# Five instead of three seven-product pairs in three gate blocks, thirteen instead of ten in the last product, with part of the weight sums added up in DRAM

## The chip, the cores and the metric

The kernel runs on one core of one Trainium2 chip. TensorE (PE in the profile, PEld its weight loads) multiplies, VectorE (DVE), ScalarE (ACT) and GpSimd (POOL) work on tiles in SBUF, and transfers are issued by SyncE (SP), ACT and POOL and carried out by the core's 16 DMA engines. The metric is the device time of one execution in microseconds; the profile is of one execution.

## The reference, cut to what matters

A two-branch decoder layer: 256 tokens, width 2048, feed-forward width 5632, all in float32.

```python
z = h @ w_in                                   # heads of both branches and two gates of 2048 columns
g_a, g_m = sigmoid(z[..., OFF_GA:OFF_GM]), sigmoid(z[..., OFF_GM:D_IN])
merged = g_a * (a_out @ w_proj_a) + g_m * (m_out @ w_proj_m)
x = x + merged @ w_out
u = causal_dwconv(rmsnorm(x) @ w_up)           # gate and value halves of 5632
x = x + (silu(u_gate) * u_val) @ w_down        # the last product: 256 x 5632 by 5632 x 2048
```

## The kernel before, in words

**Stages.** The weights are streamed once, in the order of use: the mLSTM gates (names `mog`), queries, keys and values of attention (`fq`, `fk`, `fv`), those of the mLSTM (`mq`, `mk`, `mv`), the two branch gates in four blocks of 1024 columns (`g0` to `g3`), the two projections (`p`), the output product (`wo0`, `wo1`), the up product (`up`) and the last product in two blocks of 1024 columns (`y0`, `y1`).

**A weight's way.** All weights are cut into chunks of 128 partitions by up to 2048 float32, 1 MiB at most. `load_chunk` (L124) has SP load a chunk into one of three `raw` buffers. `split_sub` (L134) splits a piece of a chunk, 1024 columns as a rule, into a high part `wh` (ACT, L170: a rounded copy) and a low part `wl` (DVE, L171: the difference); there are four buffers of each. A product is then three matmuls: low activation by `wh`, high activation by `wh`, high activation by `wl` (`prod`, L290). `next_sub` (L178) hands PE the next piece and has the pieces up to three ahead split, so a split waits for one of three things: its chunk, a free buffer, its engine.

**Pairs.** In the gate blocks, `wo` and `y`, a chunk is a pair of row blocks: 2 x 128 rows of the weight by two halves of 512 columns, a 2 x 2 matrix of blocks b12, b11, b22, b21 in the order of the chunk's columns. With the two token halves this is a 2 x 2 by 2 x 2 block product. A plain pair ("p" in the patterns of L37 to L39) takes eight products in two pieces, 24 matmuls of 512 columns. A pair of kind "S" takes Strassen-Winograd's seven products, 21 matmuls, from four pieces of 1024, 512, 1024 and 1024 columns: `b` (b11, b22), `b21`, `t13` and `t24`. For it DVE makes four sums of weight blocks in a tile `sums` (L155, L162, L165), and the activations have four sums of their own: for the gates `gate_sums` (L633) makes them once, from the normalised activations `hN`, into `gs` tiles; for `y` the up stage makes them (`put_sums`, L217), POOL stores them to `s_dram` (L949) and `load_sums` (L959) brings them back through POOL into two `s_ops` buffers, 768 KB for two pairs.

**Order around the change.** SP's, POOL's and the engines' queues run in order. In the `fq`/`fk` stage POOL also computes the inverse roots `qc` (L444) that DVE needs (L596); in the first gate block the same for the mLSTM heads (`nc`). The first gate block has plain pairs only, and its pieces run the tasks of the mLSTM and, at its end, `gate_sums`. In each block the last two pairs are plain, and the results of the seven products are put together on DVE during them.

Of the kernel before, what the change touches and what calls it, by code (L numbers as in the profile page):

```python
# [60 lines left out]
def trunk(ctx: ExitStack, tc: tile.TileContext, a):  # L61
# [57 lines left out]
    add_pairs(a["w_dn"], [Y_PAIRS] * 2)  # L119

# [13 lines left out]
    def split_sub(j):  # L134
        if j >= len(subs_of) or j in subs:
            return
        i, s, kind = subs_of[j]
# [3 lines left out]
        n = 512 if kind == "b21" else chunks[i][1] // 2  # L141
        raw, sums = raws[i], s_tiles.get("sums")


        if kind == "whole":
            src = raw[:, s * n : (s + 1) * n]
        elif kind == "b":
            src = raw[:, 512:1536]
# [4 lines left out]

            with tc.issue_after(last_of["wl"].ins):
                nc.vector.tensor_tensor(  # L155
                    sums[:, :1024].rearrange("p (i c) -> p i c", i=2),
                    raw[:, :512].unsqueeze(1).to_broadcast([P, 2, 512]),
                    src.rearrange("p (i c) -> p i c", i=2), ALU.subtract,
                )
        elif kind == "b21":  # L160
            src = raw[:, 1536:]
            nc.vector.tensor_tensor(sums[:, 1024:1536], raw[:, 1024:1536], sums[:, :512], ALU.subtract)  # L162
        elif kind == "t13":
            src = sums[:, :1024]
            nc.vector.tensor_tensor(sums[:, 1536:], raw[:, 1536:], sums[:, 1024:1536], ALU.subtract)  # L165
# [4 lines left out]
        nc.scalar.activation(wh[:, :n], src, AF.Copy)  # L170
        last_of["wl"] = nc.vector.tensor_tensor(  # L171
            wl[:, :n], src, wh[:, :n].bitcast(F32), ALU.subtract
        )
# [43 lines left out]
    def put_sums(src, dst, keep):  # L217

        a11, a21, a12, a22 = (src[:, i * P : (i + 1) * P] for i in range(4))
        n = 4 if keep else 3
# [4 lines left out]
        nc.vector.tensor_tensor(s1, a21, a22, ALU.add)
        nc.vector.tensor_tensor(s2, s1, a11, ALU.subtract)
        nc.vector.tensor_tensor(s4, a12, s2, ALU.subtract)
        put(dst[0], dst[1], sv)  # L230
# [52 lines left out]
    def s_block(name, pairs, s_ops, pattern, pools, dst, add=True, per_piece=0):  # L283
# [3 lines left out]
        ps, late, left = {}, [], pattern.count("S")  # L287
# [15 lines left out]
        def tt(o, x, y):  # L303
            late.append(lambda: nc.vector.tensor_tensor(o, x, y, ALU.add))

        for m, kind in enumerate(pattern):
# [34 lines left out]
            c11, c12, c21, c22 = (dst(tok, h) for tok in range(2) for h in range(2))  # L341
            u2 = scratch("u2", [P, 512])
            if add:
# [9 lines left out]
                tt(c22, c22, u3)
            else:
# [55 lines left out]
    def when_there(x):  # L410

        return nc.gpsimd.tensor_copy(mhalf[:, :1], x[:, :1].bitcast(F32))
# [204 lines left out]
    g_sums = [m for m, kind in enumerate(G_PAIRS) if kind == "S"]  # L617
# [315 lines left out]
    for j in range(NF):  # L933
# [12 lines left out]
        if Y_PAIRS[m] == "S":  # L946
# [9 lines left out]
    s_pos = [m for m, kind in enumerate(Y_PAIRS) if kind == "S"]  # L956
    ring = []

    def load_sums():  # L959

        i = len(ring) % (N_S // 2) * 12 * P
        if len(ring) < N_S:
            ring.append(a8(f"s_ops{len(ring)}", [12 * P], F32R))
            nc.gpsimd.dma_start(ring[-1], s_dram[:, i : i + 12 * P])

    def sums_of(b, m):
# [3 lines left out]
        at = [ring[r][:, q * P : (q + 1) * P] for q in range(6 * i, 6 * i + 6)]  # L970
# [92 lines left out]
```

## Time and profile before

| | |
|---|---|
| runs | 1378.11 us median of 3 (1377.85 to 1378.25) |
| profiled execution | 1378.12 us, of which its span is 1376.3 us |
| busy, share of the span | PE 99%, PEld 84%, DVE 78%, ACT 56%, POOL 3% |
| granted TensorE clock | 0.999 |
| moved by DMA | 281.76 MB: SP's queue 260.20 MB in 53.0% of the 16 engines' time, POOL's queue 20.38 MB in 4.4% |
| POOL | 73 instructions that count as busy |

The span is what the hardware profiler recorded of the program; 1.8 us of the execution lie around it. Busy PE counts time in which a matmul is under way. A row of the windows gives, for one stretch, its length, each engine's busy time with the number of instructions, the granted clock, the share of DMA time and the rate.

### The profile page before, as it was taken

The numbers are of one execution on the slowest core, as the hardware profiler recorded it, in microseconds if no ns is written. First come the engines' busy times: TensorE is split into PE (matmuls) and PEld (weight loads), VectorE is DVE, ScalarE is ACT, GpSimd is POOL, SyncE is SP. The second block draws the span as 40 slices with busy tenths as digits, with TensorE's granted clock in tenths as the row PEclk, the third lists the DMA queues.
The fourth block names the chain that finished last, engine by engine and source line by source line (L and its number), as shares of the span: only waits on it lengthen the run. The fifth ranks groups of instructions, "written<-read, shape, count | busy, mean of one in ns | idle before, by whom it ended". The sixth has DMA issues, their size and how long they took to land.

```text
span 1376.3 us, 18405 instructions
## 1 busy us (share of the span) xinstructions
PE 1368.2 (99%) x6934; PEld 1160.8 (84%) x6934; DVE 1078.2 (78%) x1539; ACT 770.9 (56%) x1102; POOL 40.9 (3%) x73
## 2 busy tenths in 40 slices
PE   9999999999999999999999999999999999999998
PEld 8878888888888888888888888888888888888887
DVE  5655766556888866899888888878888889889887
ACT  6655554445665544465756555556555556554553
POOL 2101000000000000000000000000000000000000
PEclk9999999999999999999999999999999999999999
DMA  9644554543555556465655555555555566768853
GB/s 324 237 180 166 182 206 153 172 155 132 189 209 186 215 213 231 177 231 200 210 207 192 195 195 199 203 199 198 196 195 189 205 239 222 257 241 277 298 192 120
DMA packets 44073, 281.76 MB, mean 205 GB/s; under 512 B 5008, under 2 KB 5024, under 8 KB 13264
## 3 DMA queue, kind: packets, MB, share of 16 engines
q1 hardware_dynamic: 39168, 260.20, 53.0%
q0 software_dynamic: 4672, 20.38, 4.4%
q8 instruction: 54, 0.88, 0.3%
q14 instruction: 35, 0.29, 0.1%
q10 hardware_dynamic: 144, 0.02, 0.0%
HBM read 272.45 MB, written 8.13 MB: 204 GB/s over the span
## 4 chain that ended last, share of the span: by engine, by line
PE 97%; issue 1%; DMA 1%; POOL 1%; DVE 0%; SPq 0%; ACT 0%; DVEq 0%; ACTq 0%; POOLq 0%
PE up L233 36%; PE p L233 6%; PE y1q L233 6%; PE y0q L233 6%; PE fq L233 3%; PE g0q L233 3%; PE mv L233 3%; PE fk L233 3%; PE fv L233 3%; PE wo0q L233 2%; PE g3q L233 2%; PE g2q L233 2%; PE g1q L233 2%; PE wo1q L233 2%; PE y1p L233 2%; PE y0p L233 2%
## 5 line engine op out<-in xcount | busy, mean ns | idle before, releaser
L170 ACT ACTIVATE wh<-raw 128x1024 fp32r<-128x1024 f32 (+2 forms) x496 | 498.2, 1015 | 407.2 <-PE up L233 109.6
L171 DVE TENSOR_TENSOR wl<-raw,wh 128x1024 fp32r<-128x1024 f32 (+2 forms) x496 | 574.0, 1167 | 189.5 <-ACT wh L170 184.7
L233 PE MATMUL up<-h,wh 128*128 128x512 f32 x1408 | 442.6, 396 | 0.0
L233 PEld LDWEIGHTS up<-h,wl 128*128 128x128 f32 x1408 | 264.4, 188 | 62.4
L233 PE MATMUL up<-h,wl 128*128 128x256 f32 x1408 | 276.6, 278 | 0.0
L233 PEld LDWEIGHTS up<-h,wh 128*128 128x128 f32 x1408 | 214.6, 189 | 0.4 <-DVE h L202 0.2
L170 ACT ACTIVATE wh<-sums 128x1024 fp32r<-128x1024 f32 x70 | 74.3, 1062 | 119.8 <-PE y1q L233 36.0
L171 DVE TENSOR_TENSOR wl<-sums,wh 128x1024 fp32r<-128x1024 f32 x70 | 85.5, 1221 | 43.9 <-ACT wh L170 43.8
L921 DVE SCALAR_TENSOR_TENSOR t<-u,cst,t 128x256 f32<-128x256 f32 x176 | 84.7, 481 | 3.7 <-ACT t L919 0.7
L233 PE MATMUL p<-wh,am 128*128 128x512 f32 x256 | 79.6, 392 | 0.0
L233 PE MATMUL y0q<-wh,ghl 128*128 128x512 f32 x232 | 71.5, 389 | 0.0
L233 PE MATMUL y1q<-wh,ghl 128*128 128x512 f32 x232 | 71.4, 389 | 0.0
L233 PEld LDWEIGHTS p<-wh,am 128*128 128x128 f32 x256 | 47.6, 188 | 9.7
L919 ACT ACTIVATE t<-u,cst 128x256 f32<-128x256 f32 x88 | 52.2, 593 | 1.7 <-DVE u L916 1.7
L233 PEld LDWEIGHTS y1q<-wh,ghl 128*128 128x128 f32 x232 | 43.5, 188 | 9.0
L233 PEld LDWEIGHTS y0q<-wh,ghl 128*128 128x128 f32 x232 | 43.5, 188 | 8.9
L233 PE MATMUL p<-wl,am 128*128 128x512 f32 x128 | 49.9, 390 | 0.0
L233 PE MATMUL y0q<-wl,ghl 128*128 128x512 f32 x116 | 45.1, 389 | 0.0
L233 PE MATMUL y1q<-wl,ghl 128*128 128x512 f32 x116 | 45.1, 389 | 0.0
L155 DVE TENSOR_TENSOR sums<-raw 128x1024 f32<-128x1024 f32 x35 | 42.6, 1217 | 0.0
L233 PE MATMUL mog<-wh,hT 128*128 128x348 f32 (+1 forms) x192 | 41.2, 324 | 1.3 <-ACT wh L170 0.9
L233 PE MATMUL g0q<-wh,hN 128*128 128x512 f32 x128 | 41.2, 401 | 0.0
(370 smaller groups left out, 2041.8 us busy)
## 6 DMA issues: line engine op xcount, KB each, us to landing
raw<-in_w_up SPq DMA_DIRECT2D x88, 1024.0 KB, 4.8
raw<-in_w_dn SPq DMA_DIRECT2D x44, 1024.0 KB, 5.2
raw<-in_w_g SPq DMA_DIRECT2D x32, 1024.0 KB, 4.8
raw<-in_w_fox SPq DMA_DIRECT2D x24, 1024.0 KB, 4.9
raw<-in_w_p SPq DMA_DIRECT2D x16, 1024.0 KB, 4.9
raw<-in_w_out SPq DMA_DIRECT2D x16, 1024.0 KB, 4.8
raw<-in_w_mqk SPq DMA_DIRECT2D x8, 1024.0 KB, 4.8
raw<-in_w_mv SPq DMA_DIRECT2D x8, 1024.0 KB, 4.8
```

The lines of the kernel that those rows point to most:

```text
L155: nc.vector.tensor_tensor(sums[:, :1024].rearrange("p (i c) -> p i c", i=2), raw[:, :512].unsqueeze(1).to_broadcast([P, 2, 512]), src.rear ...
L170: nc.scalar.activation(wh[:, :n], src, AF.Copy)
L171: last_of["wl"] = nc.vector.tensor_tensor(wl[:, :n], src, wh[:, :n].bitcast(F32), ALU.subtract)
L233: last_of["mm"] = nc.tensor.matmul(out, lhsT, rhs, start=start, stop=stop)
L919: nc.scalar.activation(t, u[:, 2:], AF.Identity, scale=w[2], bias=w[3])
L921: nc.vector.scalar_tensor_tensor(out=t, in0=u[:, i : i + S], scalar=w[i], in1=t, op0=ALU.mult, op1=ALU.add)
```

## The change

The pattern of gate blocks 1 to 3 goes from `pSpSpSpp` to `pZSZSZpp`, that of `y` from `p`, ten times `Sp`, `p` to `p`, six times `SZp`, `Zpp`. "Z" is a seven-product pair like "S", with the same four pieces for PE, whose weight sums are not made by DVE: a tile `t` of 1 MiB in DRAM per pair holds them (9 for the gates, 14 for `y`, 23 in all). The pair then takes two chunks in place of one: 768 KB of the weight itself (b11, b22, b21) and 1 MiB of `t`.

`sums_in_dram` makes a `t` in six transfers from POOL's queue, DRAM to DRAM, three of which add to what stands at their destination: b12 to two quarters, b11 and b22 added to them, the first sum copied to the third quarter, b22 added, that copied to the fourth, b21 added. Each needs the landing of the one before. `plan` places them at every second chunk from the beginning of `fox` (`fq`) and of `wo`, so that a gate tile is begun every 4 chunks and a `y` tile every 6; `begin_steps` ties a place to the chunk's first split by a one-column copy on ACT (`marks`) and one on POOL (`seen`), behind which POOL issues the transfers.

The signs of the sums are turned so that they can be made by additions: DVE's instructions stay what they were, with other operations. `gate_sums` makes five sets instead of three, the fifth in the buffer `mv`. `load_sums` brings the two pairs of an `s_ops` buffer in two transfers of 384 KB.

```diff
-G_PAIRS = "pSpSpSpp"
+G_PAIRS = "pZSZSZpp"
-Y_PAIRS = "p" + "Sp" * 10 + "p"
-N_S = Y_PAIRS.count("S")
+Y_PAIRS = "p" + "SZp" * 6 + "Zpp"
+N_S = len(Y_PAIRS) - Y_PAIRS.count("p")
...
+            if kind == "Z":
+                t = dram.tile([P, 2048], F32, name=f"t{len(z_sums)}")
+                z_sums.append((t, ap[i]))
+                add_chunk(ap[i][:, 512:], 1536, (1024, 1536))
+                add_chunk(t, 2048)
+            else:
+                add_chunk(ap[i], 2048, ("b", "b21", "t13", "t24") if kind == "S" else None)
...
+    def sums_in_dram(i):
+        t, w = z_sums[i]
+        q = lambda x, n: x[:, n * 512 : (n + 1) * 512]
+        b12, b11, b22, b21 = (q(w, n) for n in range(4))
+        put_to = lambda o, x: lambda: nc.gpsimd.dma_start(o, x)
+        add_to = lambda o, x: lambda: nc.gpsimd.dma_start(o, x, accum_op=ALU.add)
+        return [
+            put_to(
+                t[:, :1024].rearrange("p (i c) -> p i c", i=2),
+                b12.unsqueeze(1).to_broadcast([P, 2, 512]),
+            ),
+            add_to(t[:, :1024], w[:, 512:1536]),
+            put_to(q(t, 2), q(t, 0)), add_to(q(t, 2), b22),
+            put_to(q(t, 3), q(t, 2)), add_to(q(t, 3), b21),
+        ]
...
+    def plan(source, name, apart):
+        c0 = next(i for i, c in enumerate(chunks) if c[2] == name)
+        mine = [i for i, (_, w) in enumerate(z_sums) if w.tensor.name == a[source].tensor.name]
+        for n, i in enumerate(mine):
+            for step in range(6):
+                c = c0 + 2 * (apart * n + step)
+                j = next(j for j, x in enumerate(subs_of) if x[0] == c)
+                steps_at.setdefault(j, []).append((i, step))
+    plan("w_g", a["w_fox"].tensor.name, 2)
+    plan("w_dn", a["w_out"].tensor.name, 3)
...
+    def begin_steps(j, x):
+        mark = marks[:, list(steps_at).index(j) :][:, :1]
+        nc.scalar.activation(mark, x[:, :1].bitcast(F32), AF.Copy)
+        with tc.issue_after(when_there(mark).ins):
+            for i, step in steps_at[j]:
+                sums_in_dram(i)[step]()
...
         nc.scalar.activation(wh[:, :n], src, AF.Copy)
+        if j in steps_at:
+            begin_steps(j, wh)
...
     def when_there(x):
-        return nc.gpsimd.tensor_copy(mhalf[:, :1], x[:, :1].bitcast(F32))
+        return nc.gpsimd.tensor_copy(seen, x[:, :1].bitcast(F32))
...
         if i % 2 == 0:
-            g_ops["tile"] = a8(f"gs{i}", [2, 2, 512], F32R)
+            last = big.tile([P, 2, 2, 512], F32R, tag="mv", name="gs4") if i == 4 else None
+            g_ops["tile"] = last or a8(f"gs{i}", [2, 2, 512], F32R)
...
-            ring.append(a8(f"s_ops{len(ring)}", [12 * P], F32R))
-            nc.gpsimd.dma_start(ring[-1], s_dram[:, i : i + 12 * P])
+            ring.append(a8(f"s_ops{len(ring)}", [2, 6 * P], F32R))
+            for n in range(2):
+                i = (2 * len(ring) - 2 + n) % N_S * 6 * P
+                nc.gpsimd.dma_start(ring[-1][:, n], s_dram[:, i : i + 6 * P])
```

Two places show how the instructions move. The first is DVE in the middle of gate block 1. Before, a plain pair's two low parts stand ahead of an "S" pair's sums and four low parts:

```order
L171 TENSOR_TENSOR wl_3310<-raw_3261,wh_3309 128x1024
L171 TENSOR_TENSOR wl_3317<-raw_3261,wh_3316 128x1024
L155 TENSOR_TENSOR sums_3142<-raw_3297 128x1024
L171 TENSOR_TENSOR wl_3328<-raw_3297,wh_3327 128x1024
L162 TENSOR_TENSOR sums_3142<-raw_3297,sums_3142 128x512
L171 TENSOR_TENSOR wl_3341<-raw_3297,wh_3340 128x512
L165 TENSOR_TENSOR sums_3142<-raw_3297,sums_3142 128x512
L171 TENSOR_TENSOR wl_3358<-sums_3142,wh_3357 128x1024
L171 TENSOR_TENSOR wl_3376<-sums_3142,wh_3375 128x1024
```

The same place now, where a "Z" pair's four low parts (from two `raw` buffers) stand ahead of the second "S" pair of the block:

```order
L228 TENSOR_TENSOR wl_3417<-raw_3380,wh_3416 128x1024
L228 TENSOR_TENSOR wl_3424<-raw_3380,wh_3423 128x512
L228 TENSOR_TENSOR wl_3434<-raw_3404,wh_3433 128x1024
L228 TENSOR_TENSOR wl_3446<-raw_3404,wh_3445 128x1024
L210 TENSOR_TENSOR sums_3371<-raw_3443 128x1024
L228 TENSOR_TENSOR wl_3457<-raw_3443,wh_3456 128x1024
L217 TENSOR_TENSOR sums_3371<-raw_3443,sums_3371 128x512
L228 TENSOR_TENSOR wl_3467<-raw_3443,wh_3466 128x512
L220 TENSOR_TENSOR sums_3371<-raw_3443,sums_3371 128x512
L228 TENSOR_TENSOR wl_3478<-sums_3371,wh_3477 128x1024
L228 TENSOR_TENSOR wl_3490<-sums_3371,wh_3489 128x1024
```

An "S" pair's seven instructions are the same; what stands ahead of them has grown from two low parts to four, for a pair that PE leaves sooner.

The second place is POOL's queue in the `fq`/`fk` stage. Before, it holds the eight inverse roots `qc` and nothing else between the constants and the mLSTM's `nc`:

```order
L429 AFFINE_SELECT sel<-sel 96x1024
L444 TENSOR_TENSOR r_126<-v,mhalf 128x2
L429 AFFINE_SELECT sel<-sel 96x1024 x2
L444 TENSOR_TENSOR qc<-qv,mhalf 128x4 x8
L444 TENSOR_TENSOR nc<-nv,mhalf 128x2 x4
```

Now the roots stand between the steps of the gate tiles (`t_75` is the first):

```order
L504 TENSOR_TENSOR qc<-qv,mhalf 128x4
L472 COPY seen<-marks 128x1
L129 DMA t_75<-in_w_g 128x512
L129 DMA t_76<-in_w_g 128x512
L504 TENSOR_TENSOR qc<-qv,mhalf 128x4
L129 DMA t_77<-in_w_g 128x1024
L472 COPY seen<-marks 128x1
L128 DMA t_76<-t_76 128x512
L128 DMA t_77<-t_77 128x512
L128 DMA t_78<-in_w_g 128x2x512
L504 TENSOR_TENSOR qc<-qv,mhalf 128x4
```

A `qc` that had POOL to itself now comes behind a wait for ACT's mark and behind additions that themselves wait for the landing of an earlier transfer. The last step of a gate tile stands two chunks into gate block 0, the last step of a `y` tile in the last fifth of the up stage.

More of the change, by code (lines that the diff above doesn't have):

```diff
@@ L91, in trunk, with add_chunk @@
     chunks, subs_of = [], []
-    def add_chunk(ap, n, pieces=("whole", "whole")):
-        subs_of.extend((len(chunks), i, kind) for i, kind in enumerate(pieces))
+    def add_chunk(ap, n, pieces=None):
+        at = 0
+        for kind in pieces or (n // 2, n):
+            own = isinstance(kind, str)
+            subs_of.append((len(chunks), kind if own else "part", None if own else slice(at, kind)))
+            at = at if own else kind
         chunks.append((ap, n, ap.tensor.name))
@@ L104, in trunk @@
     add_b(a["w_mog1"], MOG[2])
+    z_sums = []
     def add_pairs(ap, patterns):
         for i, kind in enumerate("".join(patterns)):
-            pieces = ("b", "b21", "t13", "t24") if kind == "S" else ("whole", "whole")
-            add_chunk(ap[i], 2048, pieces)
+            if kind == "Z":
[20 more added lines that the diff above has]
+        ]
     for name in ("w_fox", "w_mqk", "w_mv"):
@@ L119, in trunk @@
     add_pairs(a["w_dn"], [Y_PAIRS] * 2)
+    steps_at = {}
+    def plan(source, name, apart):
[8 more added lines that the diff above has]
+    plan("w_dn", a["w_out"].tensor.name, 3)
+    marks = const.tile([P, len(steps_at)], F32, name="marks")
+    def begin_steps(j, x):
[4 more added lines that the diff above has]
+                sums_in_dram(i)[step]()
     raws, subs, s_tiles, last_of = {}, {}, {"of": None}, {}
@@ L136, in split_sub @@
             return
-        i, s, kind = subs_of[j]
+        i, kind, cols = subs_of[j]
         load_chunk(i)
@@ L140, in split_sub @@
             put(hT[j][:, 0, :], hT[j][:, 1, :], xT[j], cst[:, C_G1 + j : C_G1 + j + 1])
-        n = 512 if kind == "b21" else chunks[i][1] // 2
+        n = 512 if kind == "b21" else cols.stop - cols.start if cols else chunks[i][1] // 2
         raw, sums = raws[i], s_tiles.get("sums")
-        if kind == "whole":
-            src = raw[:, s * n : (s + 1) * n]
+        if kind == "part":
+            src = raw[:, cols]
         elif kind == "b":
@@ L161, in split_sub @@
             src = raw[:, 1536:]
-            nc.vector.tensor_tensor(sums[:, 1024:1536], raw[:, 1024:1536], sums[:, :512], ALU.subtract)
+            nc.vector.tensor_tensor(sums[:, 1024:1536], raw[:, 1024:1536], sums[:, :512], ALU.add)
         elif kind == "t13":
             src = sums[:, :1024]
-            nc.vector.tensor_tensor(sums[:, 1536:], raw[:, 1536:], sums[:, 1024:1536], ALU.subtract)
+            nc.vector.tensor_tensor(sums[:, 1536:], raw[:, 1536:], sums[:, 1024:1536], ALU.add)
         else:
@@ L286, in s_block @@
         q = [[pools[0](f"{name}q{tok}{h}") for h in range(2)] for tok in range(2)]
-        ps, late, left = {}, [], pattern.count("S")
+        ps, late, left = {}, [], len(pattern) - pattern.count("p")
         n_s = left
@@ L301, in piece, with tt @@
             return w
-        def tt(o, x, y):
-            late.append(lambda: nc.vector.tensor_tensor(o, x, y, ALU.add))
+        def tt(o, x, y, op=ALU.add):
+            late.append(lambda: nc.vector.tensor_tensor(o, x, y, op))
         for m, kind in enumerate(pattern):
@@ L401, in trunk @@
     mhalf = const.tile([P, 8], F32, name="mhalf")
+    seen = const.tile([P, 1], F32, name="seen")
     mask_qk = const.tile([P, P], BF16, name="mask_qk")
@@ L616, in trunk @@
     _, hN_pairs = operand("hN")
-    g_sums = [m for m, kind in enumerate(G_PAIRS) if kind == "S"]
+    g_sums = [m for m, kind in enumerate(G_PAIRS) if kind != "p"]
     g_ops = {}
@@ L945, in trunk @@
         m = j // 2
-        if Y_PAIRS[m] == "S":
+        if Y_PAIRS[m] != "p":
             se = big.tile([P, 2, 3 * P], F32R, tag="mv", name=f"se{m}")
@@ L969, in sums_of @@
             load_sums()
-        at = [ring[r][:, q * P : (q + 1) * P] for q in range(6 * i, 6 * i + 6)]
+        at = [ring[r][:, i, q * P : (q + 1) * P] for q in range(6)]
         return [(g[:, 0, 0, P:], g[:, 0, 1, P:])] + [(at[c], at[3 + c]) for c in range(3)]
```

19 lines of the change are left out of this document (9 added, 10 removed).

## The prediction

> **What bounds the kernel now.** I read the page's busy times first, then its chain that ended last, then the windows by stage.
>
> ```profile
> span 1376.3 us, 18405 instructions
> PE 1368.2 (99%) x6934; PEld 1160.8 (84%) x6934; DVE 1078.2 (78%) x1539; ACT 770.9 (56%) x1102; POOL 40.9 (3%) x73
> PE 97%; issue 1%; DMA 1%; POOL 1%; DVE 0%; SPq 0%; ACT 0%; DVEq 0%; ACTq 0%; POOLq 0%
> ```
>
> PE is busy 99% of the span and is 97% of the chain: matmuls set the end, and one taken away is a gain unless another engine falls behind. Which one is near its limit is read from the windows (length, then busy PE, PEld, DVE, ACT, POOL, granted clock, DMA share, GB/s): the `fq` to `fv` stage, gate blocks 1 to 3, `up`, `y0` and `y1`.
>
> ```profile
> 46.00:192.00 146.00, 146.00 (x680) 121.27 (x680) 96.84 (x136) 79.94 (x137) 8.07 (x8) 1.00 0.55 196
> 352.00:477.00 125.00, 125.00 (x553) 103.52 (x552) 107.12 (x116) 73.22 (x83) 0.00 (x0) 1.00 0.57 207
> 650.00:1146.00 496.00, 495.79 (x2856) 432.61 (x2855) 409.40 (x662) 295.26 (x450) 9.32 (x15) 1.00 0.57 201
> 1146.00:1259.00 113.00, 113.00 (x500) 93.55 (x499) 100.67 (x111) 64.06 (x69) 3.18 (x6) 1.00 0.71 252
> 1259.00:1372.00 113.00, 112.82 (x498) 93.09 (x496) 97.81 (x106) 59.53 (x63) 2.32 (x4) 1.00 0.61 217
> ```
>
> The clock is full everywhere. DVE is second: 86% in the gate blocks, 89% in `y0`. DMA is third: 0.71 in `y0`.
>
> **What the change takes away.** The chain in order of time (start, length, what) shows two `y` pairs in a row:
>
> ```profile
> 1151.50 0.68 PE y0p L233 x3
> 1152.18 1.36 PE y0q L233 x6
> 1153.54 2.04 PE y0p L233 x9
> 1155.58 6.12 PE y0q L233 x27
> 1161.70 0.68 PE y0p L233 x3
> 1162.38 1.36 PE y0q L233 x6
> ```
>
> Nine matmuls take 2.04 us, so one is 0.2267 us; from 1151.50 to 1161.70 an "S" and a plain pair take 45 of them, 10.20 us with no gap. A plain pair (24) is 5.44 us, a seven-product pair (21) 4.76 us: each pair converted saves 0.68 us. The gates convert two pairs in three blocks, `y` three in two: 12 pairs, 36 matmuls of 512 columns, **8.16 us** off PE, half in the gates and half in `y`. The order of PE's instructions shows it too: 4764 such matmuls for 4800.
>
> **What DVE gives back in the gates.** The pace of DVE inside an "S" pair, from the timeline of `y0`:
>
> ```profile
> 1185.56 1.22 DVE L171 TENSOR_TENSOR wl<-raw,wh 128x1024 fp32r<-128x1024 f32 x1
> 1186.69 1.22 DVE L155 TENSOR_TENSOR sums<-raw 128x1024 f32<-128x1024 f32 x1
> 1187.83 1.22 DVE L171 TENSOR_TENSOR wl<-raw,wh 128x1024 fp32r<-128x1024 f32 x1
> 1188.96 0.68 DVE L162 TENSOR_TENSOR sums<-raw,sums 128x512 f32<-128x512 f32 x1
> 1189.57 0.68 DVE L171 TENSOR_TENSOR wl<-raw,wh 128x512 fp32r<-128x512 f32 x1
> 1190.17 0.68 DVE L165 TENSOR_TENSOR sums<-raw,sums 128x512 f32<-128x512 f32 x1
> 1190.77 1.22 DVE L171 TENSOR_TENSOR wl<-sums,wh 128x1024 fp32r<-128x1024 f32 x1
> ```
>
> Back to back, starts are 1.13 us apart after 1024 columns and 0.60 after 512. An "S" pair costs DVE 4 x 1.13 + 3 x 0.60 = 6.32 us, a "Z" pair 3 x 1.13 + 0.60 = 3.99, a plain pair 2.26. Before, "S" and plain make 8.6 us in PE's 10.2. Now a gate block has Z S Z S Z without a plain pair between: Z + S is 10.31 us in PE's 9.52. A lead must carry that, and it is bounded by the four buffers:
>
> ```profile
> 1186.67 0.63 ACT L170 ACTIVATE wh<-raw 128x512 fp32r<-128x512 f32 x1 [0.29 <-PE y0q L233]
> 1189.44 1.06 ACT L170 ACTIVATE wh<-sums 128x1024 fp32r<-128x1024 f32 x1 [2.14 <-PE y0q L233]
> ```
>
> A split waits for PE to leave the piece four earlier, and starts about 0.28 us after that. Put PE's start of a block's first Z pair at 0. That pair's fourth piece reuses the buffer that the plain pair leaves at 0: ACT ends it at 0.28 + 1.06 = 1.34, and DVE, which works in order, starts its low part at about 1.4 whatever it had done before. From there it never idles: 1.13, S 6.32, Z 3.99, then the second S up to its third low part, 4.06 + 1.22, ending at 18.1 us. PE wants it for the third matmul of that S's third piece: three pairs (14.28), two pieces (2.04), two matmuls (0.45), 16.8 us. DVE is **1.4 us late in each block**, 4.2 us in three; after that come Z and two plain pairs, where it recovers. Bounds: 3 us if a release takes 0.05 instead of 0.28 us, 5.4 if every pitch is 0.03 longer. I take 4.2, nearest to the rows.
>
> The same sum in `y` leaves room, since each S Z has a plain pair ahead: 12.57 us of DVE in PE's 14.96, S's third low part about 2 us early. There the gain stands.
>
> In gate block 0 two further sets of activation sums are made.
>
> ```profile
> 344.35 1.22 DVE L171 TENSOR_TENSOR wl<-raw,wh 128x1024 fp32r<-128x1024 f32 x1
> 345.49 0.68 DVE L199 TENSOR_TENSOR gs<-sv,gs 128x512 fp32r<-128x512 f32 x1
> 346.09 0.28 DVE L229 TENSOR_TENSOR sv<-gv,sv 128x128 f32<-128x128 f32 x1
> 347.29 1.21 DVE L171 TENSOR_TENSOR wl<-raw,wh 128x1024 fp32r<-128x1024 f32 x1
> ```
>
> One set is two 512-column and four 128-column operations, 2 x 0.60 + 4 x 0.2 = 2 us, so 4 us in all. The piece whose low part starts at 347.29 is the first of gate block 1, which the chain shows starting at 352.60: 4 us of lead, just used up. I count 0, up to 1.5.
>
> **What the transfers ask.** First a load of the up stage (issues, KB each, median us to landing); then DMA in `y` before (kind, packets, MB, share; issues) and the rate in 40 slices of the first 46 us, where transfers are dense:
>
> ```profile
> raw<-in_w_up SPq DMA_DIRECT2D x88, 1024.0 KB, 4.8
> ```
>
> ```profile
> q1 hardware_dynamic: 6685, 43.89, 53.1%
> q0 software_dynamic: 1712, 8.91, 12.2%
> raw<-in_w_dn SPq DMA_DIRECT2D x40, 1024.0 KB, 5.6
> s_ops<-s_dram POOLq DMA_DIRECT2D x9, 768.0 KB, 7.1
> GB/s 0 85 285 209 83 326 403 412 397 391 396 395 386 394 386 395 397 440 409 413 396 424 403 373 377 186 207 400 70 265 330 5 77 351 188 14 67 303 246 121
> ```
>
> S Z p of `y` loads 3.75 MiB of weights and sums and 0.75 MiB of `s_ops`, 4.72 MB in 14.96 us: 315 GB/s, against 390 to 440 held for twenty slices. By the same sum a chunk's slot comes free (when the chunk three earlier is split) 5 us before its split is due for S, 8 to 9 for Z and p, and a load takes 5.6 us; S may be 2 us late, by DVE's room. Cost 0. This cover goes when the rate falls to about 330 GB/s.
>
> The Trainium skill, page "DMA: Bandwidth & Descriptors", section "Where 436 GB/s comes from", puts HBM to SBUF at about 358 GB/s per core. By that figure `y` would still fit at 88%, and the sum is the same, but the first 34 us of `y1`, with another 1 MiB of `xr`, would be within some per cent of it. The slices above 390 here speak against the figure.
>
> The sums in DRAM run beside `fq` to `g0` and `wo` to `up`. Loads there (count, duration of the issue, first and last start):
>
> ```profile
> L132 SPq DMA_DIRECT2D raw<-in_w_up x88: 327/328/328, 633.9 to 1120.4; - x88
> L132 SPq DMA_DIRECT2D raw<-in_w_fox x24: 327/328/331, 44.3 to 169.8; - x24
> ```
>
> A chunk passes every 125.5 / 23 = 5.46 us in `fox` and 5.59 in `up`. A tile writes 2.10 MB per 4 chunks there (21.8 us), per 6 here. No row shows an addition in DRAM. Bounds: its bytes as a plain write's, (4.19 + 2.10) / 21.8 = 289 GB/s in `fox`; every byte read and written counted, additions reading twice, 8.4 / 21.8 = 385 GB/s, just under what the slices hold. I take the lower half, since POOL's plain transfers run at q1's pace (8.91 MB in 12.2%, 43.89 in 53.1%). A weight load may land 11 us after its issue before PE waits: its slot is free five pieces of 2.72 us, less a split, ahead. Cost 0 to 1 us, taken as 0.3, with the marks on ACT (67 one-column copies; at POOL's 0.77 us below they would be 52 us of ACT in some 740 us in which the windows show it busy 55 to 60%).
>
> POOL's queue gets 67 marks and 138 transfers, in front of DVE's `qc` too (engine, form, count, busy and mean; the wait, us in total, times, longest):
>
> ```profile
> L412 POOL COPY mhalf<-hT 128x1 f32<-128x1 f32 x1 | 0.8, 770 | 13.0 <-DVE hT L202 13.0
> L949 POOL DMA_DIRECT2D s_dram<-se x10 | 5.4, 535 | 444.2 <-DVE se L199 444.2
> DVE qc L596 <- POOL qc L444: 9.0, 8, 1.1
> ```
>
> A step ahead of a `qc` is 0.77 + 2 x 0.53 = 1.8 us, so DVE waits up to 2.9 us in place of 1.1, at eight places. Behind it stand low parts with three pieces of 2.72 us, less 2.3 for the split, 5.9 us to spare; I count 0.
>
> **Sum.** 1378.12 us (the profiled execution: span and 1.8 us around it; the runs' median, 1378.11, is the same) - 8.16 + 4.2 + 0.3 = **1374.4 us**.
>
> **Rivals.**
> - DVE keeps up in the gates. For: it was never late there before. Against: the sum above. 1378.1 - 8.2 = 1370 us. Chance 0.08.
> - The gates lose more: 1.5 us from the sums in block 0, 1.2 from a longer pitch: 1377. DVE's 86% speaks for it. 0.15: no change.
> - `y` becomes bound by transfers. At 300 GB/s S Z p takes 15.7 us for 14.96; 12 of them lose 9 us: 1383.5. It decides below about 330 GB/s. The slices speak against it; for it, loads that already take 5.6 us for 4.8 elsewhere. 0.11.
> - The additions land late. POOL's next step waits for them, `qc` behind it, DVE behind that. The spacing is 10.9 us, the room 5.9 less 1.8: from a landing of about 15 us on, each us more is a us of PE at eight places. At 16 us: 1382.4, slower. Against: POOL's loads of 768 KB land in 7.1 us, and a step's largest transfer writes 512 KB; for: no row shows an addition. 0.21.
> - That the change doesn't do what it says is excluded for PE by the 36 matmuls.
>
> The same page, section "Queues, rings and completion order", says that each DMA engine takes turns between queues packet by packet. By that rule a weight load beside the additions is stretched to about twice its transfer, some 7.5 us, within its 11, and the last rival could only come through POOL. The 5.6 us beside `s_ops` agree with it; the sum is the same.
>
> **Numbers.** Forecast 0.45, its own range 1372.8 to 1375.8. The range: 1371 (full gain just outside) to 1384 (`y` at 300 GB/s, additions landing at 16 us). A measurement of this kernel tells about 0.2%, 2.8 us, from no change: faster ends at 1375.4. Faster: 0.42 of the forecast and the 0.08; slower: 0.13 of late additions, 0.08 of `y`; same: the rest, 0.29.
>
> **What would show it.** Right: in each of gate blocks 1 to 3 PE waits about 1.4 us in all for DVE's `wl`, most of it in the second S pair, so that they stay near 41.5 us each; `y0` and `y1` each 2 us shorter without a gap; loads of `t` landing in 5 to 6 us; `qc` waits under 3 us. Wrong: PE waiting for `raw` by way of ACT in `y`, additions landing after 10 us, or gate blocks of 40 us.

## The result, and the profile after

The changed kernel takes 1385.45 us (median of 5 runs, 1383.83 to 1386.59) where the kernel before takes 1378.11: ratio 1.0053, 95% interval 1.0042 to 1.0064. It is slower by half a per cent, and outside the range of the prediction. A second measurement of the same kernel (`e9_after_again`, below) gave 1383.78 us (1381.02 to 1385.40), ratio 1.0037, 1.0025 to 1.0050; that median would lie just inside the range. The runs of each spread over 3 to 4 us; those of the kernel before over 0.4 us beside the first. One run of `e5_y1_paced` (the profiled one, at a mean granted clock of 0.654), one of `e8_all_four` and one of the kernel before beside e9 to e11 took 1938, 2279 and 4069 us, and the ratios leave these three out.

The profiled execution took 1383.83 us, the shortest of the five. First the page: span and engines, DMA queues (packets, MB, share of 16 engines), chain by engine.

```profile
span 1381.7 us, 18798 instructions
...
PE 1366.8 (99%) x6898; PEld 1155.6 (84%) x6898; DVE 1083.7 (78%) x1557; ACT 795.9 (58%) x1198; POOL 200.0 (14%) x297
...
q1 hardware_dynamic: 42480, 278.28, 54.7%
q0 software_dynamic: 24336, 72.16, 26.3%
...
PE 91%; DVE 3%; DMA 3%; ACT 1%; issue 1%; POOL 0%; ACTq 0%; DVEq 0%; SPq 0%; POOLq 0%
```

The 36 instructions of PE are gone, but the chain, which was 97% PE, is now 91% PE, and 3% of it, some 40 us, runs through DMA. The windows of the stages `fq` to `fv`, gates 1 to 3, `up`, and the start of `y1` (length, busy PE, PEld, DVE, ACT, POOL, clock, DMA share, GB/s) show where that can be:

```profile
46.00:192.00 146.00, 144.67 (x674) 119.91 (x673) 95.68 (x135) 79.94 (x149) 45.21 (x52) 1.00 0.94 260
352.00:477.00 125.00, 123.40 (x535) 99.12 (x534) 114.79 (x130) 82.34 (x99) 0.00 (x0) 1.00 0.73 261
650.00:1146.00 496.00, 493.28 (x2830) 430.18 (x2829) 411.67 (x674) 299.15 (x487) 80.92 (x124) 1.00 0.87 252
...
1268.00:1296.00 28.00, 25.81 (x110) 19.85 (x108) 20.86 (x22) 15.57 (x17) 5.38 (x10) 1.00 1.00 362
```

The DMA engines, busy 0.55 and 0.57 of the time before in the first and third stage, are at 0.94 and 0.87, at rates of 250 to 260 GB/s: busy, but not with many bytes. At the start of `y1` they are at 1.00.

Stage lengths from PE's timeline (first matmul of a stage to the first of the next; `y1` to the start of the last matmul; the third column reaches from `wo1` to the 201st matmul of `up`), us. The other stages agree within 0.15 us.

| kernel | `fk` | gates 1 to 3 | `wo1` to `up` | `y0` | `y1` |
|---|---|---|---|---|---|
| before | 45.49 | 124.44 | 80.96 | 112.89 | 112.65 |
| 36 matmuls fewer, no stall | 45.49 | 120.36 | 80.96 | 110.85 | 110.61 |
| after | 47.03 | 124.57 | 84.99 | 110.87 | 114.99 |
| lost, after | 1.5 | 4.2 | 4.0 | 0.0 | 4.4 |

Of the 8.16 us saved, 4.2 are given back in the gates, as forecast; another 9.9 us go in three places where 0.3 us was forecast in all: 14.1 lost less 8.2 saved is 5.9 us, and the profiled executions differ by 5.7.

The chain in order of time shows what these three places wait for. In `fk` (start, length, what):

```profile
111.86 13.76 DMA raw<-in_w_fox
...
125.72 1.06 ACT wh L225
...
128.60 1.23 DVE wl L228
129.83 0.09 DVE qv L503
...
129.99 1.04 POOL qc L504
...
131.06 0.24 DVE qc L656
...
131.33 0.70 DVE qn L658
...
132.07 0.66 PE ps_k L642 x4
```

One weight load takes 13.76 us (4.9 at the median before). ACT's split waits for it, DVE's low part for ACT, and behind that low part, in DVE's order, stands `qv`, on which the transposes `ps_k` hang. PE does not run out of weights here; it waits for a small operation that is queued behind a late split. Between `wo1` and `up` it is the same:

```profile
641.75 8.27 DMA raw<-in_w_up
...
650.12 1.07 ACT wh L225
...
651.22 1.23 DVE wl L228
652.45 0.60 DVE u L361
...
654.24 1.20 DVE x L958 x2
...
658.04 0.66 PE ps_h L937 x4
```

The load of 8.27 us holds a low part, behind which DVE has the sums of the output product (`u`, `x`); the transposes `ps_h`, and with them the first operands of `up`, wait for those. The load before it, issued at 635.34 us, had taken 10.98 us and had already held ACT, and DVE behind it, for longer (in brackets the wait):

```profile
646.43 1.06 ACT L225 ACTIVATE wh<-raw 128x1024 fp32r<-128x1024 f32 x1 [4.06 <-DMA raw<-in_w_up]
650.12 1.06 ACT L225 ACTIVATE wh<-raw 128x1024 fp32r<-128x1024 f32 x1 [2.40 <-DMA raw<-in_w_up]
```

Not all of the 4.0 us lost here is waiting. Right behind it the granted clock is one half for 3.4 us, and PE, busy all the time, gets through 12 matmuls where the next 3.4 us have 21 (columns as in the windows above, the clock third from the end):

```profile
658.60:662.00 3.40, 3.40 (x12) 2.82 (x12) 3.09 (x8) 3.40 (x10) 0.22 (x1) 0.50 0.85 255
662.00:665.40 3.40, 3.40 (x21) 3.00 (x20) 2.13 (x4) 2.32 (x5) 0.00 (x0) 1.00 1.01 407
```

That is about 1.5 us, an estimate from 12 matmuls for 21; the rest is PE's wait. At the start of `y1` PE waits for the splits themselves:

```profile
1272.88 9.64 DMA raw<-in_w_dn
...
1282.63 1.07 ACT wh L225
...
1286.83 7.11 DMA raw<-in_w_dn
...
1294.04 1.07 ACT wh L225
```

### The profile page after: what moved, and what is told of

It is laid out like the page before. It is cut to its first block, busy times and chain, and to the rows that moved or that the text cites. A ratio compares the mean times of both kernels' runs of the same rounds, so it can differ in the third digit from the quotient of the medians.

```text
span 1381.7 us, 18798 instructions
## 1 busy us (share of the span) xinstructions
PE 1366.8 (99%) x6898; PEld 1155.6 (84%) x6898; DVE 1083.7 (78%) x1557; ACT 795.9 (58%) x1198; POOL 200.0 (14%) x297
## 3 DMA queue, kind: packets, MB, share of 16 engines
q1 hardware_dynamic: 42480, 278.28, 54.7%
q0 software_dynamic: 24336, 72.16, 26.3%
## 4 chain that ended last, share of the span: by engine, by line
PE 91%; DVE 3%; DMA 3%; ACT 1%; issue 1%; POOL 0%; ACTq 0%; DVEq 0%; SPq 0%; POOLq 0%
PE up L290 36%; PE p L290 6%; PE y0q L290 5%; PE y1q L290 4%; PE mog L290 3%; PE mv L290 3%; PE fv L290 3%; PE fq L290 3%; PE y0p L290 3%; PE wo0q L290 2%; PE g2q L290 2%; PE g3q L290 2%; PE y1p L290 2%; PE g1q L290 2%; PE mk L290 2%; PE mq L290 2%
## 5 line engine op out<-in xcount | busy, mean ns | idle before, releaser
L225 ACT ACTIVATE wh<-raw 128x1024 fp32r<-128x1024 f32 (+3 forms) x542 | 537.9, 1008 | 444.5 <-PE up L290 135.7
L228 DVE TENSOR_TENSOR wl<-raw,wh 128x1024 fp32r<-128x1024 f32 (+3 forms) x542 | 621.9, 1161 | 208.6 <-ACT wh L225 201.4
L472 POOL COPY seen<-marks 128x1 f32<-128x1 f32 x67 | 50.4, 752 | 481.7 <-ACT marks L171 481.7
L225 ACT ACTIVATE wh<-sums 128x1024 fp32r<-128x1024 f32 x48 | 50.9, 1061 | 65.7 <-DVE sums L220 17.3
L228 DVE TENSOR_TENSOR wl<-sums,wh 128x1024 fp32r<-128x1024 f32 x48 | 58.7, 1222 | 15.5 <-ACT wh L225 14.6
L290 PE MATMUL y1q<-wh,ghl 128*128 128x512 f32 x196 | 60.5, 390 | 0.0
L290 PE MATMUL y0q<-wh,ghl 128*128 128x512 f32 x196 | 60.4, 389 | 0.0
L290 PEld LDWEIGHTS y1q<-wh,ghl 128*128 128x128 f32 x196 | 36.7, 188 | 7.8 <-ACT wh L225 0.3
L290 PE MATMUL mv<-wh,hT 128*128 128x512 f32 x128 | 40.2, 395 | 0.0
L290 PE MATMUL fq<-wh,hT 128*128 128x512 f32 x128 | 40.0, 394 | 0.0
```

Of the source, the lines that this page charges most:

```text
L228: last_of["wl"] = nc.vector.tensor_tensor(wl[:, :n], src, wh[:, :n].bitcast(F32), ALU.subtract)
L290: last_of["mm"] = nc.tensor.matmul(out, lhsT, rhs, start=start, stop=stop)
L472: return nc.gpsimd.tensor_copy(seen, x[:, :1].bitcast(F32))
```

## The experiments

The question is what makes those loads late: the sums in DRAM (theory 1), for `y1` the transfers that POOL issues there (theory 2), and for the gates whether DVE is the cause (theory 3). Stage lengths of all runs stand in one table at the end of this section. Each ratio is to the kernel before on the same chip.

### The sums in DRAM: none, copies only, marks only, another place

`e1_no_sums`:

```diff
-                add_chunk(t, 2048)
+                add_chunk(ap[i], 2048)
...
-    plan("w_g", a["w_fox"].tensor.name, 2)
-    plan("w_dn", a["w_out"].tensor.name, 3)
```

> Leaves out the sums of weights in DRAM: the second load of each Z pair takes the weights again instead of t, in as many bytes, and no copy, addition, mark or wait of theirs is left. Theory 1 (the traffic of the sums beside the weight loads delays these loads, 1.5 us in fq and fk and 4.1 us between the output product and the up product): about 5.5 us come back, 1380 us, with the loads of the up product back from 7.5 us to about 5 us at the median, and the loss of about 4.4 us at the start of y1 stays. Rival A (the whole loss comes from the loads in y and from DVE in the gates, and the sums only move it about): 1384 to 1386 us.

1379.03 us, ratio 1.0008 (0.9999 to 1.0017). `fk` and `wo1` to `up` are back at the lengths of before to 0.01 us. Queues and two groups of loads of this kernel (KB each, median us to landing):

```profile
q1 hardware_dynamic: 42480, 278.28, 56.5%
q0 software_dynamic: 7408, 23.92, 5.2%
...
raw<-in_w_up SPq DMA_DIRECT2D x88, 1024.0 KB, 4.9
...
raw<-in_w_fox SPq DMA_DIRECT2D x24, 1024.0 KB, 4.8
```

With the same bytes for the weights, loads land in 4.8 and 4.9 us, against 8.3 (`fox`) and 7.5 (`up`) in the change. `y1` keeps its loss: 116.53 us, more than in the change, with a stretch of half the granted clock in it (1280.2 to 1283.6 us), which the change's `y1` has not. The two places belong to the sums, the third doesn't.

`e12_marks_only` (second load of Z as in e1):

```diff
-            for i, step in steps_at[j]:
-                sums_in_dram(i)[step]()
+            nc.gpsimd.tensor_copy(seen, mark)
```

> As e1_no_sums, but all marks of ACT and the waits of POOL for them stay, each followed by one more small copy on POOL where the transfers were; the copies and additions in DRAM are left out and the second load of each Z pair takes the weights again. Tells apart what e1 took away together. If the traffic delays the weights, the time is e1's, 1378 to 1380 us, with no gap of PE at 130 and 654 us. If POOL's and ACT's extra waits delay what stands behind them (the qc of fq and fk, the loads of x and the stores of xs at the output product), 1.5 us at fq and fk or 2.5 to 5 us ahead of the up product stay: 1380.5 to 1384 us.

1379.16 us, ratio 1.0008 (0.9999 to 1.0017), and `fk` and `up` as before: the marks on ACT and the waits in POOL's queue cost nothing that can be measured. It is the transfers.

`e2_copies`:

```diff
-        add_to = lambda o, x: lambda: nc.gpsimd.dma_start(o, x, accum_op=ALU.add)
+        add_to = lambda o, x: lambda: nc.gpsimd.dma_start(o, x)
```

> The four additions of each Z pair become plain copies of the same shapes (the sums are then not computed); marks, waits, order and the number of transfers stay. If the adding itself is what makes the transfers heavy (q0's share of the DMA engines 26.3% for 72 MB), q0 falls to under 15% and about 4 of the 5.5 us that e1 gives come back: about 1381 us. If it is the number of transfers and the waits of POOL and ACT around them, the time stays at 1384 to 1386 us with gaps of PE at the same places.

1384.29 us, ratio 1.0040 (1.0027 to 1.0052). Neither theory has it quite: the time is that of the second, but the share of POOL's queue fell, to 20.6%, and one of the two stalls went.

```profile
q0 software_dynamic: 21392, 72.16, 20.6%
```

In `fk` there is no stall now (45.49 us), between `wo1` and `up` there is (85.58). So adding is dearer than copying, and copies between two places in DRAM already take much of the DMA engines. (A tile has three additions, not four as expected here: 512, 256 and 256 KB, half of what is written.)

`e7_sums_in_up` (`plan` has a third argument, the number of loads after the first of that weight at which the first step stands):

```diff
-    plan("w_dn", a["w_out"].tensor.name, 3)
+    plan("w_dn", a["w_up"].tensor.name, 2.5, 6)
```

> The sums of w_dn start with the seventh load of w_up instead of the first of w_out, one step of a pair every 2 loads and a new pair every 5 loads instead of 6, so that none of them lies beside the output product and the start of the up product; the same transfers in all. Theory 1: the two gaps of PE among the ps_h transposes go, up's first matmuls come 2.6 to 4.1 us earlier against the output product, steady up stays at 139.3 us for 800 matmuls, and 3 to 4.5 us come back: 1380.5 to 1382.5 us. Rival D (beside the up product, with more transfers at a time, they delay weights as much): steady up longer by 2 us or more, time at 1384 us or above.

1378.87 us, ratio 1.0006 (0.9997 to 1.0015), better than expected; `wo1` to `up` takes 80.97 us, as before. The DMA view from 630 to 660 us, first of the change, then of e7:

```profile
q0 software_dynamic: 715, 2.04, 47.3%
q1 hardware_dynamic: 672, 4.85, 43.5%
...
raw<-in_w_up SPq DMA_DIRECT2D x4, 1024.0 KB, 9.6
```

```profile
q1 hardware_dynamic: 720, 5.24, 50.7%
q0 software_dynamic: 257, 0.97, 8.4%
...
raw<-in_w_up SPq DMA_DIRECT2D x4, 1024.0 KB, 5.3
```

In the change POOL's queue took more of the engines' time for 2.04 MB than SP's for 4.85. Beside the up product, where the same additions now stand more densely (one tile per 5 loads instead of 6), they cost nothing: 455.62 us from the 201st matmul of `up` to `y0`, in both kernels.

### The start of `y1`

`e3_xr_late`:

```diff
+        if b == 1 and m == 8:
+            nc.gpsimd.dma_start(xrs[1], xs[:, :, 1024:2048])
```

> The 1 MiB load of xr1 is issued by POOL with the sums of pair 8 of y1 instead of ahead of y1; nothing else moves. Theory 2 (at the start of y1 xr1, two rings of s_ops and the weights together ask for more than the DMA engines give, and weights come late): the gaps of PE at 1282 to 1296 us go, 3 to 4.4 us come back, 1381 to 1382.5 us. Rival B (the two rings and the second load of the Z pairs do it alone): under 1 us comes back, 1384.5 to 1385.5 us, with loads of 8 to 10 us and gaps at the same place.

1382.44 us, ratio 1.0034 (1.0023 to 1.0045), `y1` 114.76 us. This run tested nothing: nothing held the load back, so POOL's queue kept its order. POOL's timeline of e3 (start, length, what, wait ahead of it):

```profile
1271.41 0.70 POOL L1033 DMA_DIRECT2D xr<-xs  x1 [28.51 <-DVE wl L228]
1273.20 2.14 POOL L1026 DMA_DIRECT2D s_ops<-s_dram  x4 [1.09 <-PE y1p L290]
1284.08 1.05 POOL L1026 DMA_DIRECT2D s_ops<-s_dram  x2 [8.74 <-PE y1q L290]
1291.38 1.06 POOL L1026 DMA_DIRECT2D s_ops<-s_dram  x2 [6.25 <-PE y1p L290]
1296.88 1.05 POOL L1026 DMA_DIRECT2D s_ops<-s_dram  x2 [4.44 <-PE y1q L290]
```

It counts as a repeat of the change, and shows the pattern at issue: `xr1` and five `s_ops` buffers, 4.75 MiB, in 27 us. In `y1` the tiles that hold the activations of `y` come free as pairs are done, the `s_ops` buffers take their place, and POOL fills each at once: the last of them 34 us into `y1`, where e10 below fills it 71 us into `y1` and PE never waits for it.

`e5_y1_paced`, where a load waits for a mark that ACT writes:

```diff
+    def paced(m, f):
+        mark = y_marks[:, m : m + 1]
+        nc.scalar.activation(mark, last_of["wh"][:, :1].bitcast(F32), AF.Copy)
+        with tc.issue_after(when_there(mark).ins):
+            f()
...
+            paced(m, load_ring) if b else load_ring()
...
+        if b == 1 and m == 14:
+            paced(30, lambda: nc.gpsimd.dma_start(xrs[1], xs[:, :, 1024:2048]))
```

> In y1 alone, each ring of sums waits on POOL for a mark that ACT writes when the split has come to that ring's pair, and xr1 waits for the mark of pair 14; so POOL no longer issues xr1 and two rings together when y0's outputs have left. e3 did not test this: POOL took xr1 and the rings in the same order and at the same time as before. Theory 2 (at the start of y1, xr1 and rings that are not needed for another 15 to 30 us take the DMA engines from the weights): the gaps of PE at 1276 to 1296 us go, y1 takes 110.5 to 111.2 us from its first matmul to the last instead of 115.0, and the time is 1379.5 to 1381.5 us. Rival B (the two loads of each Z pair, 1.75 MiB in the time of one pair, are enough by themselves): y1 stays at 114 us or more, and the time at 1383 to 1385.5 us.

1377.60 us, ratio 0.9998 (0.9989 to 1.0007): 6 us under the change, more than `y1` had lost, so part of it may be the spread of the other places. The stage lengths with this pacing are read from e8 and e10, which have the same `y1`: 110.62 us, all of the loss gone.

`e6_rings_paced` (the `s_ops` buffers, called rings in the expectations, paced, `xr1` where the change has it) and `e11_xr_paced` (only `xr1` paced) share it out:

> As e5, but xr1 stays where the change has it, ahead of y1's rings. Tells how the loss at the start of y1 is shared: if the rings crowd the weights, nearly all of it goes (y1 in 111 to 112 us, time 1380 to 1382.5 us); if xr1 does, under 1.5 us goes (y1 in 113.5 to 115 us, 1383 to 1385 us).

> Only xr1 waits for a mark (that of pair 14 of y1); the rings are as in the change. If the loss at the start of y1 comes from POOL, which stands at xr1 until y0's outputs have left and then issues xr1 and two rings at once, taking xr1 out of the way lets the rings go as their buffers come free, and the loss goes as in e5: y1 in 110.5 to 111.5 us, time 2.5 to 4.5 us under that of e9. If the rings that run ahead take the transfers whether xr1 is there or not, y1 stays at 113 to 115 us and the time within 1.5 us of e9's.

e6: 1379.46 us (ratio 1.0008, 0.9999 to 1.0017), `y1` 113.70. e11: 1378.76 us (1.0007, 0.9998 to 1.0016), `y1` 111.93. So neither alone does it: of 4.4 us, 3.1 stay with `xr1` early, 1.3 with the rings early. Each share is from one execution, e6's the longest of its ten and e11's the shortest of its eleven, so they are rough. The reason given ahead of e11, that POOL's wait for `xr1` bunches the rings, falls: with `xr1` out of the way they came just as bunched, four transfers from 1268.47 us on.

### The gates

`e4_gate_order`:

```diff
-G_PAIRS = "pZSZSZpp"
+G_PAIRS = "pZSpZSZp"
```

> Gate blocks 1 to 3 take the pairs as pZSpZSZp instead of pZSZSZpp: the same number of products, splits and sums, with a plain pair between the two S. Theory 3 (DVE falls behind because Z S Z S Z gives it more work than PE takes time, and 4 buffers of wh and wl don't bridge that): PE's wait of about 1.1 us in each gate block falls under 0.4 us and blocks of 41.5 us become 40.4 to 40.8 us: 2 to 3.3 us back, 1382 to 1383.5 us. Rival C (the wait in the gates is for weights, late by the sums in DRAM): blocks stay at 41.4 us or longer and the time at 1385 to 1386 us.

1383.35 us, ratio 1.0036 (1.0023 to 1.0049). Less than expected: the gates take 123.84 us instead of 124.57, and blocks 2 and 3 41.0 us, where 40.1 would be without a stall. The waits of PE's weight loads (PEld) in these blocks are for DVE's `wl` (us in total, times, longest), two per "S"; block 3, and block 2 has the same:

```profile
PEld g3p L290 <- DVE wl L228: 1.4, 4, 0.4
```

So theory 3 holds as to the engine, but a plain pair between the two "S" is not enough while each "S" still stands right behind a "Z".

### Together

`e8_all_four` takes the pacing of e5, the plan of e7, the order of e4, and one gate tile per 6 loads (`plan("w_g", ..., 3)`).

> The pacing of e5, the plan of e7, the gate order of e4, and the sums of w_g a new pair every 6 loads instead of every 4 (2 transfers at a time instead of 3). If the three causes add up, it is after less 4 (y1), less 3 to 4 (start of up), less 1 to 3 (gates), less 1 (fq, fk): 1371.5 to 1376 us, faster than the kernel before. If the causes share one reserve and each only passes its wait on: 1378 to 1381 us.

1377.07 us, ratio 0.9993 (0.9984 to 1.0002): less than the causes add up to. `fk`, `up` and `y1` are free of stalls (45.39, 80.98, 110.62), `fk` with the gate tiles begun every 6 loads instead of 4, but the sums of the gates now run into gate block 1, where the "Z" pairs load 1.75 MiB each, and this block takes 46.04 us (the load in the chain: start, length):

```profile
369.54 8.90 DMA raw<-in_w_g
```

`e10_combined` is e8 with these sums begun 3 loads ahead of `fox` and ended before block 1, and with each "S" behind a plain pair (the diff is to the change):

```diff
-G_PAIRS = "pZSZSZpp"
+G_PAIRS = "pSZpSZZp"
...
-    plan("w_g", a["w_fox"].tensor.name, 2)
+    plan("w_g", a["w_fox"].tensor.name, 2.5, -3)
```

> As e8_all_four, with the gate pairs as pSZpSZZp (each S behind a plain pair, as in the last product, where S shows no stall) and the sums of w_g begun three loads before w_fox, a new pair every 5 loads, so that they end before gate block 1. e8 lost 4.6 us in gate block 1 alone, where additions ran beside the loads of its Z pairs. Theory 3 in the form that e4 leaves (an S right behind a Z costs 0.36 us, since DVE has no plain pair to catch up in): gate blocks 2 and 3 take 40.1 to 40.4 us instead of 40.9 to 41.0, and gate block 1 about 41.2. Sum: 1377.07 - 4.6 - 1.2 = about 1371.5; forecast 1370.5 to 1374 us, faster than the kernel before. Rival: additions beside fq and fk cost the 1 to 1.5 us again that they cost in the change, 1373 to 1375.5 us; or S is too much for DVE wherever it stands, 1372.5 to 1374 us with gaps of 0.1 us behind each S.

**1370.49 us** (1370.07 to 1371.65), ratio 0.9947 (0.9933 to 0.9960): faster than both kernels. The gates take 121.70 us (40.94, 40.16 and 40.60, where 40.1 would be without a stall); the one wait that PE's timeline still shows in them is 0.49 us for `wl` in block 1, and in block 3 PE's weight loads wait 0.5 us for ACT's `wh`. Windows of e10, the same stages:

```profile
46.00:192.00 146.00, 146.00 (x680) 121.32 (x679) 95.56 (x135) 83.65 (x162) 59.95 (x63) 1.00 0.91 264
650.00:1142.00 492.00, 491.78 (x2824) 429.03 (x2824) 409.45 (x671) 298.93 (x516) 107.86 (x174) 1.00 0.89 262
1259.00:1287.00 28.00, 28.00 (x125) 23.17 (x125) 26.24 (x27) 19.02 (x22) 3.24 (x6) 1.00 0.86 310
```

The DMA engines are nearly as busy as in the change (0.91 and 0.89 for 0.94 and 0.87), yet PE is busy throughout. In these runs what counts is not the share over a stage but whether dense transfers meet a place where the split has little lead.

`e9_after_again` is the changed kernel itself beside these two:

> The changed kernel itself, unchanged, beside the next two on one chip. e3, whose order on every queue was that of the change, gave 1382.44 us (1380.67 to 1385.34) where the change had given 1385.45 (1383.83 to 1386.59); if waits for late transfers make up its loss, its time spreads over some 4 us and its median lies anywhere between: 1382 to 1386 us, with gaps of PE at 130, 654 and 1277 to 1296 us again. If it is under 1380 us, the verdict on the change itself has to be told anew.

1383.78 us; the three losses again.

| kernel | time, us | `fk` | gates 1 to 3 | `wo1` to `up` | `y0` | `y1` |
|---|---|---|---|---|---|---|
| after, again (e9) | 1383.78 | 46.92 | 124.59 | 86.25 | 110.94 | 115.65 |
| e3, order as after | 1382.44 | 46.85 | 124.50 | 86.07 | 110.93 | 114.76 |
| e1 no sums | 1379.03 | 45.49 | 124.58 | 80.96 | 110.87 | 116.53 |
| e12 marks only | 1379.16 | 45.49 | 124.55 | 80.92 | 110.90 | 117.36 |
| e2 copies | 1384.29 | 45.49 | 124.54 | 85.58 | 110.87 | 114.44 |
| e7 sums in `up` | 1378.87 | 47.41 | 124.55 | 80.97 | 110.87 | 114.63 |
| e6 rings paced | 1379.46 | 46.39 | 124.58 | 87.09 | 110.94 | 113.70 |
| e11 `xr1` paced | 1378.76 | 45.90 | 124.58 | 82.95 | 110.87 | 111.93 |
| e4 gate order | 1383.35 | 47.28 | 123.84 | 83.23 | 110.87 | 114.37 |
| e8 all four | 1377.07 | 45.39 | 127.92 | 80.98 | 111.10 | 110.62 |
| e10 combined | 1370.49 | 45.39 | 121.70 | 81.01 | 110.86 | 110.62 |

Times are medians, stage lengths those of one profiled execution. Where the sums stand as in the change, `wo1` to `up` lies anywhere from 82.95 to 87.09 us, and the granted clock sorts these: it does not fall in e11 and e4 (82.95, 83.23), it is one half for 3.4 us in the change and e9 (84.99, 86.25) and for 6.8 us in e3 and e6 (86.07, 87.09). The kernel's runs spread with it too: e9's shortest, 1381.02 us, had a mean granted clock of 1.000, its longest, 1385.40, of 0.997; the change's 0.999 at 1383.83 and 0.997 at the median, 1385.45.

## Why the prediction was wrong, point by point

**8.16 us off PE: right.** `y0` is 2.02 us shorter without a stall (2.04 expected), and e10, nearly rid of its stalls, is 7.6 us under the kernel before (0.6 us of it in the first 55 us, which differ by as much from profile to profile).

**4.2 us back in the gates: right in sum, not in its parts, and so in part by luck.** Measured 4.2. Blocks 2 and 3 lose 1.12 and 1.07 us (1.4 forecast), block 1 loses 2.0, 0.64 of it at its start, where PE waits for DVE's `am`, which stands in DVE's chain behind operations of the activation sums (two sets more, costed at 0 with a bound of 1.5; that they cause it is argued, not shown, and e10, with as many sets, has no such wait). The rest is DVE being late, as worked out: its timeline of the change in block 3 has no idle time from 444.85 to 473 us, and the low part that the sum puts at 18.1 us behind PE's start of the first "Z" pair (442.75 us) ends 17.9 us behind it, at 460.67. What PE waits for differs. In the first "S" of the block, where the sum has no wait, PE's weight loads already wait 0.7 us for `wl`. In the second it is not the third piece's low part: PE takes that piece's high part and then wants the fourth piece's, which ACT can only make from DVE's third sum (L220). DVE's timeline, then the chain:

```profile
458.84 0.69 DVE L220 TENSOR_TENSOR sums<-raw,sums 128x512 f32<-128x512 f32 x1
459.45 2.52 DVE L228 TENSOR_TENSOR wl<-sums,wh 128x1024 fp32r<-128x1024 f32 x2
```

```profile
459.65 1.07 ACT wh L225
460.76 1.20 PE g3p L290 x4
```

The loss of blocks 2 and 3 stays in e1, e2 and e12, whatever the traffic, and with the order of e10 falls to 0.05 and 0.5 us: that DVE's place in the order is the cause is shown.

**"Cost 0 to 1 us, taken as 0.3" for the sums in DRAM: wrong; they cost 5.5 us.** Two steps failed, and a third cost wasn't in the sum. The first step was the price of an addition. Between its bytes as a plain write's and every byte read and written, the prediction said "I take the lower half, since POOL's plain transfers run at q1's pace". Here POOL's queue took 26.3% of 1381.7 us, 363 us, for 72.16 MB; without the sums (e1) 5.2% of 1377.5, 72 us, for 23.92. So the 48.24 MB of the sums cost 292 us of all 16 engines, 165 GB/s, where SP's 278.28 MB in 54.7% went at 368. At these means a gate tile, 2.10 MB, takes 12.7 us and its four loads 11.4: 24.1 us of DMA in a spacing of 21.8. The prediction's upper bound, 385 GB/s, "just under what the slices hold", was the nearer end, and it was summed too low: with the tile's bytes read, written and, for additions, read again, 2.10 + 2.10 + 1.05 MB, and 4.19 of loads, it is 9.4 MB in 21.8 us, 433 GB/s, over what the slices hold. The row that set the price moved no data from DRAM to DRAM.

The second was the room: "A weight load may land 11 us after its issue before PE waits". That is PE's room for the weights. The chains above show another path: the split stands in DVE's order ahead of `qv` and of the sums behind `wo1`, and these had less room, so that two loads of 10.98 and 8.27 us, neither over those 11 us, stopped PE between `wo1` and `up`. The third cost is the clock: "The clock is full everywhere" held for the kernel before, but behind the stall at `up` it fell to one half, about 1.5 of the 5.5 us.

The prediction weighed the Trainium skill, page "DMA: Bandwidth & Descriptors", section "Queues, rings and completion order": the engines take turns between queues by packets, so that a load beside the additions would be stretched to about twice its transfer, an estimate of some 7.5 us. The medians are near it (7.5 us in `up`, 8.3 in `fox`); it was the loads above the median, and the places with less room, that cost the time.

**"`qc` waits under 3 us": right, and so the rival of late additions had the right sign by a wrong path.** It held that additions landing from about 15 us on would stop POOL, and POOL the roots. The transfers of 512 KB into the tiles landed in 9.5 and 10.2 us at the median (`w_dn` and `w_g`), at the 10 us that the prediction gave as a sign of being wrong, and single ones in up to 17.6; but DVE's longest wait for a `qc` was 1.3 us:

```profile
DVE qc L656 <- POOL qc L504: 9.4, 8, 1.3
```

e12 excludes that path. The rival that was missing is the plain one: the sums make the weight loads late.

**"Cost 0" for the transfers of `y`: right for `y0`, wrong for the start of `y1` (4.4 us).** The sum was made for the steady S Z p, and there it holds. For "the first 34 us of `y1`, with another 1 MiB of `xr`" the prediction saw the danger, and set it aside on the slices above 390 GB/s. As a rate they were about right: the twenty slices run from 326 to 440, not from 390, but 22 us of the kernel before moved 399 GB/s, and the change moves 403 in the middle of the stall (one window of each, the rate last):

```profile
7.00:29.00 22.00, 21.06 (x128) 20.04 (x128) 13.63 (x21) 14.62 (x29) 7.59 (x18) 1.00 1.03 399
```

```profile
1276.00:1290.00 14.00, 11.93 (x50) 8.87 (x50) 9.10 (x10) 5.93 (x8) 1.05 (x2) 1.00 1.08 403
```

So the figure of the Trainium skill, page "DMA: Bandwidth & Descriptors", section "Where 436 GB/s comes from" (about 358 GB/s), is no limit that these traces bear out, though the 28 us from 1268 us on, with a slower start, come to 362. What was counted too low is the demand: five `s_ops` buffers came in the time of two. With `xr1` they are 4.98 MB in 27 us, 184 GB/s, beside 263 for the weights (3.93 MB in 14.96 us), some 445 GB/s together, an estimate, and more than either stretch moved. e5, e6, e8 and e11 show both parts.

**The range** ended at 1384 with one mechanism at a time. Here two that were held to be free cost 5.5 and 4.4 us together with the gates' 4.2: 1378.1 - 8.2 + 4.2 + 5.5 + 4.4 = 1384.0, where the profiled execution took 1383.8.

## What to carry to other kernels

Work that is moved to DMA engines with time to spare is priced in the time that the engines are busy, from a row of the same kind of transfer, not in bytes at the rate of the weights; and it is placed away from stage boundaries and from stages that load densely: the same additions cost 4 us between two products and nothing in the middle of the longer one. A load has room only up to the first thing queued behind its split on any engine, not up to the matmul that uses it. And transfers that a free buffer releases run ahead of their need: tie them to the progress of the work. When runs begin to spread, read the granted clock in short windows: PE at half the clock does not show in its busy time.

## What the runs showed of the hardware

- Bytes moved from DRAM to DRAM by POOL's queue are dear in DMA time. Plain copies (e2): 20.6% of 1380.0 us less the 72 us of the other transfers is 213 us for 48.24 MB, 227 GB/s. If the half of the bytes that are copies in the change cost as much there, the additions are left with 292 - 106 = 186 us for 24.12 MB, an estimate of 130 GB/s: 2.8 times the DMA time of a weight load per byte.
- A busy share of the DMA engines tells little of waits: at 0.91 over 146 us (e10, `fq` to `fv`) PE never waited, at 0.92 over 28 us it was idle for 2.7 of them (the change, 630 to 658 us):

```profile
630.00:658.00 28.00, 25.32 (x124) 20.97 (x122) 23.88 (x31) 14.70 (x25) 7.51 (x10) 1.00 0.92 241
```

- A stall of PE can cost more than its length. In seven of the twelve profiles of kernels with the change whose stages are given above, the granted clock fell to 0.50 for 3.4 or 6.8 us during or right behind a stall (the change, e2, e3, e6 and e9 at 657 to 659 us, e9 again at 1286.8, e1 and e12 at 1280 to 1281). Stalls of much the same length left it full (2.05 us ahead of `ps_h` in e4 and e11); what decides it no run shows.
